# Batched experts MLP on one core: which engine waits at the end for the stores

## The chip, the cores and the metric

The kernel runs on one core of one Trainium2 chip. The metric is the device time of one execution in microseconds; a few executions of the same program are timed, and the median is given. One further execution is recorded by the hardware profiler.

A core has five engines, each with an instruction sequencer of its own: TensorE (PE: matmuls, and PEld: its weight loads), VectorE (DVE), ScalarE (ACT), GpSimd (POOL) and SyncE (SP). They run independently and wait for each other through semaphores. In the profile a "q" behind an engine's name marks an instruction that the sequencer alone handles, such as a wait; PE's are listed as PEldq.

## The reference

Eight experts, each a two-layer network with a ReLU between, on its own 256 rows:

```python
n_experts, capacity, hidden, expert_hidden = 8, 256, 512, 2048
x  : (n_experts, capacity, hidden)        float32
w1 : (n_experts, hidden, expert_hidden)   float32
w2 : (n_experts, expert_hidden, hidden)   float32

h = np.matmul(x, w1)
h = np.maximum(h, 0)
return np.matmul(h, w2).astype(np.float32)
```

## The kernel before

The kernel writes each engine's instruction stream by hand, with semaphores of its own. Weights and half of the rows are turned into bfloat16 on their way in by the DMAs that POOL issues.

**PE** first transposes the rows of x, in four rounds of 16 transposes (line 256). Then it runs a loop of four passes (line 259), two experts a pass. A pass computes the first layer of both experts (line 272), four blocks of four 128-wide slices of the 2048, and then the second layer of both (line 292), 16 slices of 128 by two halves of the 256 rows, into one PSUM tensor `pt_o`. The loop is the last thing in PE's stream.

**DVE and ACT** share the work behind PE by halves: ReLU from PSUM to `ht_sb` (lines 219 and 221), and the copy of each finished half of an expert's output from `pt_o` to `out_sb` (line 228). They report their copies on `s_dve` and `s_act`.

**POOL** issues the loads of the weights, each one expert ahead of its use as buffers come free. When the copies of the first four experts are done, it issues one store of their output (line 167, semaphore `s_out[0]`), and then drains (line 168).

**SP** issues two loads of x at the start. After that it passes the landings of the weights on to PE (lines 116 to 124). At the end it waits for the copies of experts 4 to 6 and issues one store for the three (line 126, `s_out[1]`), then for those of expert 7 and issues the last store (line 128, `s_out[2]`). At the end of the program's text, in lines 302 and 303, it waits for the landings of the three stores, each of which adds 16 to its semaphore:

```python
    for s in s_out:
        sp.wait_ge(s, 16)
```

Nothing follows in the kernel on any engine. In the built program the three waits are two instructions: one for `s_out[1]`, and one for `s_out[2]` and `s_out[0]` together. Semaphores appear in the trace by number: `s_out[0]` to `s_out[2]` are S[103] to S[105], `s_act` and `s_dve` are S[125] and S[126], and S[131] and S[132] tell ACT and DVE that a half of the second layer is complete.

The wait of line 88, which appears in the profile for PE, is in a helper, `take`, that waits for a semaphore and lowers it.

Of the kernel before, what the change touches and what calls it, by code (L numbers as in the profile page):

```python
# [9 lines left out]
def kernel(  # L10
# [74 lines left out]
    sp, pool, act, dve, pe = nc.sync, nc.gpsimd, nc.scalar, nc.vector, nc.tensor  # L85
# [214 lines left out]
                        ins.then_inc((s_ob, s_oa)[m], 1)  # L300

    for s in s_out:
        sp.wait_ge(s, 16)


# [28 lines left out]
```

## Time and profile before

| | |
|---|---|
| median of 3 runs | 179.55 us |
| lowest, highest | 179.49, 179.88 us |
| the profiled execution's own time | 179.56 us |
| its span, first to last instruction of the kernel | 178.2 us |
| PE busy | 130.0 us (73%) |
| DVE, ACT, POOL busy | 37.5, 37.9, 12.9 us |
| DMA, mean over the span | 229 GB/s |
| mean granted clock of TensorE | 0.966 |

The span is that of the kernel's own instructions, whichever engine has the first and the last. The execution's time is counted outside it and is longer. In the profile's lists a row gives the engine, the source line, the operation and the tensors (output, an arrow, inputs), then a count and times; a wait is given as who waited, an arrow, and what ended the wait. The list of DMA issues gives the KB of each and the time from issue to landing.

### The profile page before, as it was taken

The numbers are of one execution on the slowest core, as the hardware profiler recorded it, in microseconds if no ns is written. First come the engines' busy times: TensorE is split into PE (matmuls) and PEld (weight loads), VectorE is DVE, ScalarE is ACT, GpSimd is POOL, SyncE is SP. The second block draws the span as 40 slices with busy tenths as digits, with TensorE's granted clock in tenths as the row PEclk, the third lists the DMA queues.
The fourth block names the chain that finished last, engine by engine and source line by source line (L and its number), as shares of the span: only waits on it lengthen the run. The fifth ranks groups of instructions, "written<-read, shape, count | busy, mean of one in ns | idle before, by whom it ended". The sixth has DMA issues, their size and how long they took to land. (4 is left out here: it accounts for less than half of the span.)

```text
span 178.2 us, 2354 instructions
## 1 busy us (share of the span) xinstructions
PE 130.0 (73%) x824; PEld 88.8 (50%) x832; DVE 37.5 (21%) x48; ACT 37.9 (21%) x49; POOL 12.9 (7%) x27
## 2 busy tenths in 40 slices
PE   0034479898939297888769695979496698999880
PEld 0033378785414196773224485954142587964330
DVE  0134654331010133330100231320101113420110
ACT  2465554231010122130100122220101022220110
POOL 3600000101010101000000101010201200000000
PEclk9999999999999999999979999999999569999997
DMA  6999999999999998998999999999999999999998
GB/s 224 333 237 206 232 210 206 232 213 202 235 213 199 235 221 191 235 224 188 235 224 202 221 224 213 210 232 210 206 232 210 206 232 196 209 224 208 263 422 364
DMA packets 4240, 40.90 MB, mean 229 GB/s; under 512 B 400, under 2 KB 400, under 8 KB 1936
## 3 DMA queue, kind: packets, MB, share of 16 engines
q0 software_dynamic: 3408, 37.23, 95.2%
q1 hardware_dynamic: 832, 3.67, 5.2%
HBM read 71.30 MB, written 4.19 MB: 424 GB/s over the span
## 5 line engine op out<-in xcount | busy, mean ns | idle before, releaser
L272 PE MATMUL pt_h<-xe,w_sb 128*128 x512 | 65.1, 284 | 12.9 <-PEq L88 12.7
L272 PEld LDWEIGHTS pt_h<-xe,w_sb 128*128 x512 | 57.4, 147 | 21.2 <-issue 19.4
L292 PE MATMUL pt_o<-w_sb,ht_sb 128*128 x248 | 57.8, 387 | 12.5 <-PEq L88 12.1
L292 PEld LDWEIGHTS pt_o<-w_sb,ht_sb 128*128 x256 | 24.9, 99 | 44.2 <-issue 16.8
L221 DVE TENSOR_SCALAR ht_sb<-pt_h 128x512 bf16<-128x512 f32 x32 | 22.2, 693 | 52.0 <-PE pt_h L272 52.0
L219 ACT ACTIVATE ht_sb<-pt_h 128x512 bf16<-128x512 f32 x32 | 19.2, 600 | 56.9 <-PE pt_h L272 56.9
L256 PE MATMUL pt_tr<-identity,x_b 128*128 128x128 bf16 x64 | 7.5, 309 | 17.7 <-PEq L88 17.7
L228 DVE COPY out_sb<-pt_o 128x512 f32 x8 | 5.5, 692 | 67.2 <-PE pt_o L292 67.2
L228 ACT COPY out_sb<-pt_o 128x512 f32 x8 | 4.7, 585 | 65.4 <-PE pt_o L292 65.4
L256 PEld LDWEIGHTS pt_tr<-identity,x_b 128*128 128x128 bf16 x64 | 6.5, 143 | 18.4 <-issue 18.4
L132 POOL DMA_DIRECT2D w_sb<-in_w_dram x8 | 4.9, 616 | 69.9 <-ACTq L223 69.9
L198 DVE COPY xe<-pt_tr 128x1024 bf16<-128x1024 bf16 x3 | 6.2, 2077 | 8.1 <-PE pt_tr L256 8.1
L198 ACT COPY xe<-pt_tr 128x1024 bf16<-128x1024 bf16 x3 | 6.3, 2088 | 6.1 <-PE pt_tr L256 6.1
L137 POOL DMA_DIRECT2D w_sb<-in_w_dram x6 | 3.2, 536 | 36.3 <-ACT out_sb L228 36.2
L178 ACT CAST x_b<-x_f 128x1024 bf16<-128x1024 f32 x2 | 4.0, 1982 | 2.8 <-DMA x_f<-in_x_dram 2.8
L178 DVE CAST x_b<-x_f 128x1024 bf16<-128x1024 f32 x2 | 2.1, 1062 | 4.1 <-DMA x_f<-in_x_dram 4.1
L139 POOL DMA_DIRECT2D w_sb<-in_w_dram x2 | 1.1, 528 | 17.1 <-ACT out_sb L228 17.1
L178 ACT COPY x_b<-x_c 128x1024 bf16<-128x1024 bf16 x2 | 2.2, 1119 | 0.0
L178 ACT ACT_TABLE_LOAD x1 | 1.3, 1283 | 2.5 <-PEq L99 2.5
L194 DVE COPY xe<-pt_tr 128x1024 bf16<-128x1024 bf16 x1 | 0.7, 692 | 4.6 <-PE pt_tr L256 4.6
L194 ACT COPY xe<-pt_tr 128x1024 bf16<-128x1024 bf16 x1 | 1.0, 1012 | 2.0 <-PE pt_tr L256 2.0
L178 DVE COPY x_b<-x_c 128x1024 bf16<-128x1024 bf16 x2 | 1.4, 692 | 0.0
(10 smaller groups left out, 4.0 us busy)
## 6 DMA issues: line engine op xcount, KB each, us to landing
w_sb<-in_w_dram POOLq DMA_DIRECT2D x14, 2048.0 KB, 29.8
w_sb<-in_w_dram POOLq DMA_DIRECT2D x2, 1152.0 KB, 26.4
out_dram<-out_sb POOLq DMA_DIRECT2D x1, 2048.0 KB, 35.9
w_sb<-in_w_dram POOLq DMA_DIRECT2D x2, 896.0 KB, 30.2
out_dram<-out_sb SPq DMA_DIRECT2D x1, 1536.0 KB, 8.8
x_f<-in_x_dram SPq DMA_DIRECT2D x1, 1024.0 KB, 5.4
x_c<-in_x_dram POOLq DMA_DIRECT2D x1, 1024.0 KB, 9.4
x_f<-in_x_dram SPq DMA_DIRECT2D x1, 512.0 KB, 3.3
```

The costliest lines, as they stand in the source:

```text
L132: pool.dma_start(w1_k[:, e % 2 * KT1:(e % 2 + 1) * KT1], w1_r[e]).then_inc(s_w1[e], 16)
L137: pool.dma_start(w2_k[:, k:k + KT2], w2_r[e]).then_inc(s_w2[e], 16)
L139: pool.dma_start(w2_k[:, k:k + CUT], w2_r[e, :, :CUT]).then_inc(s_w2[e], 16)
L178: copy(x_b[:, b].rearrange("p (t m) q -> p t m q", m=MT), src.rearrange("p m (q t) -> p t m q", t=KT1),).then_inc(t_xb, 1)
L194: copy(xe[:, a * n:(a + 1) * n], pt[b][:].rearrange("p j q -> p (j q)")).then_inc(s_xe[b], 1)
L198: copy(xl[:, :, :, :, a - e0].rearrange("p l j q -> p j l q"), pt[b][:].rearrange("p j (l q) -> p j l q", l=l),).then_inc(s_xe[b], 1)
L219: act.activation(dst, ph[half][:], relu).then_inc(t_h, 1)
L221: dve.tensor_relu(dst, ph[half][:]).then_inc(t_h, 1)
L228: copy(outs[b], po[:, half]).then_inc(s_copied, 1)
L256: ins = pe.transpose(pt[b][:, j], x_b[:, b, j], identity[:])
L272: ins = pe.matmul(ph[i // 2][:, i % 2, :], ws[i % 2 * KT1 + kt], xs[kt], start=(kt == 0), stop=(kt == KT1 - 1),)
L292: ins = pe.matmul(po[:, m], hs[(kt - k0) * MT + m], ws[kt - k0], start=(kt == 0), stop=(kt == KT2 - 1),)
```

## The change

The waits for the landings of the three stores at the end of the program move from SP's stream to PE's. On SP the issue of the last store (line 128) is then the last instruction of the kernel; on PE the two wait instructions follow the end of the loop of line 259.

```diff
                         ins.then_inc((s_ob, s_oa)[m], 1)
 
     for s in s_out:
-        sp.wait_ge(s, 16)
+        pe.wait_ge(s, 16)
```

## The prediction

> **What bounds the kernel now.** I read the head of the profile page first, then its chain that ended last, then the waits of SP's own queue, because the change touches only what comes after the last store.
>
> ```profile
> span 178.2 us, 2354 instructions
> PE 4%; ACT 0%; issue 0%
> PE pt_o L292 4%; ACT out_sb L228 0%
> ```
>
> ```profile
> engine line waited for: us in total, times, longest us
> SPq L116 <- DMA w_sb<-in_w_dram: 87.5, 8, 20.3
> ...
> SPq L303 <- DMA out_dram<-out_sb: 4.1, 2, 3.1
> ```
>
> The chain stops at the last copy and covers only 4% of the span: it does not show the tail that matters here. The waits of SP's queue do. SP sits in line 303, the waits that the change moves, for 4.1 us in two pieces, and a DMA out of out_sb ends both. The timeline of the last stretch gives the order:
>
> ```profile
> 165.98 7.07 PE L292 MATMUL pt_o<-w_sb,ht_sb 128*128 x31 [0.79 <-PEq L88]
> 168.32 0.40 SPq L126 DMA_DIRECT2D out_dram<-out_sb  x1
> 172.87 0.69 DVE L228 COPY out_sb<-pt_o 128x512 f32 x1 [7.16 <-PE pt_o L292]
> 173.09 0.58 ACT L228 COPY out_sb<-pt_o 128x512 f32 x1 [7.27 <-PE pt_o L292]
> 173.70 0.35 SPq L128 DMA_DIRECT2D out_dram<-out_sb  x1
> ```
>
> ```profile
> out_dram<-out_sb SPq DMA_DIRECT2D x1, 1536.0 KB, 8.8
> ...
> out_dram<-out_sb SPq DMA_DIRECT2D x1, 512.0 KB, 4.5
> ```
>
> PE's last product is out at 165.98 + 7.07 = 173.05 us, the last copy at 173.67, and SP issues the last store at 173.70. It lands 4.5 us later, at 178.2, and that is the span's end. So the body of the kernel ends on a landing, and no engine that waits for it can change when it comes. Only two things are left to the change: how fast the waiting engine notices, and what follows the wait.
>
> What follows is small but not nothing. The profiled execution took 179.56 us against a span of 178.2 (178.212 in the trace), so some 1.35 us lie around the span. The views of the profile page stop at the span's end; the trace's list of semaphore updates does not. Semaphore 2, which no line of the kernel names, is updated there in two rounds of nine:
>
> ```
> S[2] round 1, us: 173.227 173.789 175.739 175.783 178.336 178.379 178.418 178.452 178.499
> S[2] round 2, us: 179.326 179.360 179.399 179.442 179.465 179.564 179.603 179.637 179.684
> between: S[207]-S[255] from 178.464, S[156]-S[206] from 178.519, S[105]-S[155] from 178.564,
>          S[54]-S[104] from 178.567, S[7]-S[53] from 178.719 to 179.067 (all set back)
> landings of the last store (S[105]): 177.880 first, 178.167 last, 16 in all
> before: S[131] 173.063 (last matmul), S[125] 173.679 (last ACT copy)
> ```
>
> I read round 1 as a closing barrier that passes through five engines and back: 173.227 comes 0.164 after PE's last matmul, 173.789 comes 0.110 after ACT's last copy, 175.739 follows the end of POOL's drain (below), 175.783 is DVE, and 178.336 is SP, after its last wait. Then four steps back. So PE stands at the head of the chain and SP at its turning point. The owners are my inference from these neighbours; the list gives no engine. [...]
>
> **The change part by part.** No transfer, copy or matmul is touched. Two sequencer instructions leave SP's end (three waits fold into two: one for the 1536 KB store, one for the other two together) and stand at PE's end.
>
> *Whom the new wait holds up.* On PE nothing of the kernel is queued behind it. In front of it stand the matmuls, and PE's sequencer is long past them:
>
> ```profile
> L259 PEldq ALU_OP  x4: 36/36/36, 55.2 to 169.2; - x4
> L259 PEldq COMPARE_BRANCH  x4: 67/214/214, 55.3 to 169.3; - x4
> ```
>
> The last loop branch is issued at 169.3, nearly 9 us before the landing, so reaching the wait costs nothing: those 9 us hide it. If the cover were gone, it would be the branch's 0.067 us. SP, once it has issued the store (173.70 + 0.35), has nothing left but its part in the barrier. POOL could be a later step in PE's chain:
>
> ```profile
> L168 POOLq DRAIN  x1: 36825/36825/36825, 138.4 to 138.4; - x1
> ```
>
> Its drain runs from 138.370 (138.4 in the row) for 36.825 us, to 175.195, and its update follows 0.544 later, at 175.739. That is 2.4 us before the last landing, so POOL is ready when PE arrives: nothing.
>
> *Noticing the landing.* The price of a wait on each sequencer, from the barrier at the start and PE's own takes:
>
> ```profile
> L303 SPq EVENT_SEMAPHORE  x2: 17/22/28, 177.1 to 178.2; - x2
> ...
> L88 PEldq EVENT_SEMAPHORE  x92: 51/51/51, 8.6 to 168.2; - x92
> ```
>
> SP's last wait begins 17 ns after the last landing (178.184 against 178.167) and takes 28 ns for two semaphores, where one takes 17. On PE one takes 51. No row has PE waiting for two: I add SP's difference, 28 - 17 = 11, for 62 (between 51 and 51 x 28/17 = 84). PE also notices later: at the start barrier a release at 0.644 begins SP's wait instruction at 0.660 and PE's at 0.673, 13 ns more. Together (62 - 28) + 13 = +47 ns, bounds +36 and +69.
>
> *From the wait to the barrier.* SP's update came 178.336 - 178.212 = 124 ns after its wait ended. For PE there are two rows: 164 ns from its last matmul to its update in round 1, where its sequencer had run ahead and only the array was late, and 179.326 - 179.067 = 259 ns from its last set-back semaphore to its update in round 2, where the sequencer itself was last. After the change the sequencer is what is late, so I take 259: 259 - 124 = +135 ns, bounds +40 and +135.
>
> *The way through the chain.* With SP last, four steps follow its update: 178.499 - 178.336 = 163 ns. With PE last, all eight follow. Round 2 is that case, as PE sets back its semaphores last: 179.684 - 179.326 = 358 ns, eight steps. So 358 - 163 = +195 ns (139 for the four steps forward; the other 56 is the turn, 99 instead of 43). It is measured, and only its place is argued; bounds +139 to +195. [...] The trace's steps are 23 to 99 ns, and the trace is used.
>
> *After the chain.* PE is the last to be let go in both cases, sets back its semaphores slowest, and opens round 2: nothing changes.
>
> Sum: 47 + 135 + 195 = +377 ns. Against the profiled execution 179.56 + 0.38 = 179.94 us. The median of the three runs, 179.55, stands 0.01 below that execution, so the forecast is 179.94 either way: slower by 0.21%. The bounds add up to 36 + 40 + 139 = +0.22 and 69 + 135 + 195 = +0.40, so 179.78 to 179.96. A measurement of this kernel can tell about 0.2%, 0.36 us, from no change: the forecast sits just over that line.
>
> **The rivals.**
>
> *PE is as quick as SP (not slower by what can be told).* [...] As a mechanism of this kernel: if the 51 ns are mostly a record that overlaps the next instruction, and the 259 ns the tail of the set-backs, only the chain is left, +0.195, and the time is 179.56 + 0.20 = 179.76. For it: PE's ordinary register operation takes 36 ns, quoted above, no triple of anything. Against: 51 ns in all 92 of its waits, to SP's 17 to 28. It decides when PE's exit takes under 240 ns, for then the sum drops below 0.36. Chance 0.17.
>
> *The rim is constant.* If what lies outside the span does not depend on who comes last (another order in the chain, or a clock that stops elsewhere), only the +47 ns inside the span remain: 179.61. For it: no view shows the rim. Against: 178.212 plus the list's 1.47 us is about the time that was counted. Chance 0.10.
>
> *A slow exit.* POOL's way from its drain's end to its update was 0.544 us. If PE, held in a wait rather than running through, needs as long in place of 259, the time is 179.94 + 0.29 = 180.23. Nothing but that row speaks for it. Chance 0.13.
>
> *Faster.* SP would have to be the slow one to leave, and its 124 ns is less than any PE row; what is left is that the stores land earlier than in this execution. The three runs' lowest lies 0.07 below the profiled one: 179.49, within the line. A gain over 0.36 us needs an earlier landing, and no edit touches a transfer. Chance 0.05.
>
> That the change does not do what it says can be left aside: the diff moves exactly the waits on the three store semaphores, and no store remains without one.
>
> **How the numbers follow.** The forecast has 0.55. With the runs' scatter (179.49 to 179.88) on top of its bounds it ends above 0.36 us in about three of four cases: 0.41 slower and 0.14 same. The slow exit adds 0.13 to slower, 0.54. Quick PE and constant rim add 0.27 to same, 0.41. Faster 0.05. The range has to hold the constant rim at 179.61 and the slow exit at 180.23: 179.6 to 180.25, which leaves out the faster case and the tails. The forecast's own range is 179.78 to 179.96.
>
> **What would show it.** In the changed kernel's profile the rows of line 303 should stand under PE's sequencer, two of them, at 51 ns or a little more, the last beginning some 30 ns after the last landing, and SP's waits for that line gone. The span should be 178.2 + 0.05 with the landing where it was. In the semaphore list round 1 should start only after the landing, with all nine updates in one run of about 0.36 us. Time outside the span should grow from 1.35 to about 1.68. I am wrong if the rim stays at 1.35, if round 1 still has its first updates at 173, or if the last store's 4.5 us to landing moves by more than the whole effect.

## The result and the profile after

The changed kernel takes 179.83 us (median of 20 runs, 179.69 to 180.09) against 179.59 for the kernel before (20 runs, 179.49 to 179.88). The ratio is 1.0014, 95% interval [1.0008, 1.002]: slower by 0.24 us. That is clear of no change in this many runs, and smaller than the 0.36 us that the prediction drew as its line.

The body of the kernel did what it did. The last stretch of the changed kernel's timeline, and the line of the last store in its list of DMA issues:

```profile
165.87 7.07 PE L292 MATMUL pt_o<-w_sb,ht_sb 128*128 x31 [0.79 <-PEq L88]
168.53 0.40 SPq L126 DMA_DIRECT2D out_dram<-out_sb  x1
172.76 0.69 DVE L228 COPY out_sb<-pt_o 128x512 f32 x1 [7.17 <-PE pt_o L292]
172.97 0.58 ACT L228 COPY out_sb<-pt_o 128x512 f32 x1 [7.27 <-PE pt_o L292]
173.58 0.35 SPq L128 DMA_DIRECT2D out_dram<-out_sb  x1
```

```profile
out_dram<-out_sb SPq DMA_DIRECT2D x1, 512.0 KB, 4.8
```

The last store is issued 0.11 us earlier than in the profile before, and lands 4.8 us later in place of 4.5. This move of 0.35 us is more than the whole effect, which the prediction had named as a sign of being wrong. It is the luck of this execution, whose own time was 180.08 us, 0.25 above the changed kernel's median: in the nine traces of this case the store is issued between 172.35 and 173.98 us, takes 4.17 to 5.77 us, and lands between 178.08 and 178.41. Comparing the two profiled executions by their ends would therefore mislead. Measured from the last landing, the luck drops out, so every reading below starts there.

Two rows by source line show that the wait moved and what it costs on PE, and that POOL's drain was over long before, at 138.3 + 37.0 = 175.3:

```profile
L303 PEldq EVENT_SEMAPHORE  x2: 51/51/51, 177.2 to 178.4; - x2
```

```profile
L168 POOLq DRAIN  x1: 36997/36997/36997, 138.3 to 138.3; - x1
```

In the waits of SP's queue no row of line 303 is left. The longest waits are these, and the waits for the weights are as before:

```profile
SPq L116 <- DMA w_sb<-in_w_dram: 87.4, 8, 20.3
SPq L103 <- DVE out_sb L228: 34.9, 5, 7.7
SPq L121 <- DMA w_sb<-in_w_dram: 34.8, 6, 9.7
```

The trace's list of semaphore updates shows the rest, as it did before:

```
changed kernel, us
last landing of the last store (S[105]): 178.405
PE's last wait: begins 178.434, ends 178.485
S[2] round 1: 178.677 178.711 178.750 178.794 178.817 178.916 178.955 178.989 179.036
S[2] round 2: 179.854 179.888 179.926 179.971 179.994 180.092 180.131 180.165 180.211
```

Round 1 no longer starts at 173. All nine updates come after the landing, in one run of 0.359 us. From the last landing to the last update of round 2 it is 180.211 - 178.405 = 1.806 us, against 179.684 - 178.167 = 1.517 before: +0.289. That tail of 0.29 and a landing that came 0.24 later account for the 0.52 us between the two profiled executions.

The counted time follows this list: the profiled execution's own time lies 0.124 us below its last update before the change, 0.131 after, and 0.114 to 0.137 in the seven experiments. So whatever delays the last update lengthens the time, although no view of the page shows these updates.

One trace of each kernel is little, but the time outside the span, in which the landing has no part, is on record for every execution (with the span to 0.1 us). Its mean is 1.57 us over the 20 of the changed kernel, and 1.32 and 1.33 over 28 and 19 executions of the kernel before, taken beside the experiments. That is +0.24 to +0.25, and the two traces give 1.595 - 1.348 = +0.25. The mean span is 178.28 us against 178.26 and 178.30.

### The profile page after: what moved, and what is told of

Read it like the earlier page. It is cut to its first block, busy times and chain, and to the rows that moved or that the text cites. A ratio compares the mean times of both kernels' runs of the same rounds, so it can differ in the third digit from the quotient of the medians.

```text
span 178.5 us, 2354 instructions
## 1 busy us (share of the span) xinstructions
PE 131.2 (74%) x824; PEld 89.7 (50%) x832; DVE 37.5 (21%) x48; ACT 37.9 (21%) x49; POOL 12.7 (7%) x27
## 5 line engine op out<-in xcount | busy, mean ns | idle before, releaser
L272 PE MATMUL pt_h<-xe,w_sb 128*128 x512 | 66.3, 288 | 11.7 <-PEq L88 11.5
L272 PEld LDWEIGHTS pt_h<-xe,w_sb 128*128 x512 | 58.3, 147 | 20.3 <-issue 17.6
```

The source lines that it names most:

```text
L272: ins = pe.matmul(ph[i // 2][:, i % 2, :], ws[i % 2 * KT1 + kt], xs[kt], start=(kt == 0), stop=(kt == KT1 - 1),)
```

## The experiments

The theory: the program ends with a barrier that passes through PE, ACT, POOL, DVE and SP and back. An engine that is late for its turn costs its own exit, and every step of the chain that then remains. Two rivals: PE costs because its sequencer is slow, wherever it stands; or SP is special, and any other engine costs the same.

**PE waits for the first two stores, SP for the last.** It undoes the part of the change that matters if order decides.

```diff
-    for s in s_out:
-        pe.wait_ge(s, 16)
+    for s in s_out[:2]:
+        pe.wait_ge(s, 16)
+    sp.wait_ge(s_out[2], 16)
```

> PE waits for the first two stores, SP alone for the last. The closing chain theory (PE heads a barrier that passes PE, ACT, POOL, DVE, SP and back; only an engine late for its turn costs, and the later its place the fewer steps follow): PE leaves its wait near 177.2, a microsecond before the last landing, the chain reaches SP before SP is free, and the time is that of before, 179.59, with the last update of semaphore 2 some 1.52 us after the last landing. The rival, that a wait on PE costs because PE leaves the kernel slowly wherever it stands, expects part of the 0.24 us that the change cost: 179.7 or more.

Measured: 179.55 against 179.54 us for the kernel before in the same runs, ratio 0.9999 [0.999, 1.0008]. PE's wait for the two earlier stores begins at 177.0 and SP's for the last at 178.2:

```profile
L303 PEldq EVENT_SEMAPHORE  x1: 51/51/51, 177.0 to 177.0; - x1
```

```profile
L304 SPq EVENT_SEMAPHORE  x1: 17/17/17, 178.2 to 178.2; - x1
```

In the list, four updates follow PE's wait and stop at SP, and five come when SP is free:

```
last landing 178.143; S[2] round 1: 177.211 177.245 177.284 177.328 | 178.295 178.339 178.377 178.411 178.458
```

The interval alone would still allow +0.14 us, a part of the 0.24. The tail does not: it is 178.143 to 179.639, 1.496 us, against 1.517 before. Nor does the time outside the span, with a mean of 1.33 us over 11 executions against 1.32 over 28. A wait on PE costs nothing as long as PE is not the last. The rival that it always costs falls.

**ACT, DVE or POOL waits in place of SP.** Three kernels, each with one word changed:

```diff
     for s in s_out:
-        sp.wait_ge(s, 16)
+        act.wait_ge(s, 16)     # second kernel: dve, third: pool
```

> ACT waits for the three stores in place of SP. Chain theory: ACT is second, so three steps forward (39 + 43 + 23 = 105 ns) and the slower turn (56 ns) come on top of SP's case, and ACT's own wait and exit cost as SP's do: +0.16 us, 179.75, and 1.68 us from the last landing to the last update of semaphore 2 (1.52 before, 1.81 with PE). Rival, PE's slow sequencer alone (51 ns a wait against ACT's and SP's 17): ACT costs nothing, 179.59. Second rival, SP is special and any other engine costs the same: +0.24 as PE, 179.83.

> DVE waits for the three stores. Chain theory: DVE stands just ahead of SP, so one step forward (23 ns) and the slower turn (56 ns) are added, and about 40 ns for its slower wait and exit: +0.12 us, 179.71, 1.64 us from the last landing to the last update. Slow-sequencer rival: a few ns (21 a wait), 179.6. SP-is-special rival: 179.83.

> POOL waits for the three stores after its drain. Chain theory with POOL's own exit as the trace of before has it (0.544 us from its drain's end to its update, 0.42 more than SP's 0.124): two steps forward (43 + 23) and the turn (56) make 0.122, so +0.54 us, 180.13, 2.06 us from the last landing to the last update. If those 0.544 us belong to the drain and not to the exit, +0.12: 179.71. SP-is-special rival: 179.83.

Measured, against 179.54 us in the same runs: ACT 179.75, ratio 1.0011 [1.0002, 1.002]; DVE 179.68, 1.0008 [0.9999, 1.0017], which by itself does not tell it from no change (the time outside the span does: a mean of 1.44 us over 11 executions against 1.32 over 28, where a single execution scatters by 0.03 to 0.04); POOL 180.15, 1.0032 [1.002, 1.0044]. The rows of line 303, in this order:

```profile
L303 ACTq EVENT_SEMAPHORE  x2: 17/28/38, 176.9 to 178.1; - x2
```

```profile
L303 DVEq EVENT_SEMAPHORE  x2: 21/36/50, 176.9 to 178.2; - x2
```

```profile
L303 POOLq EVENT_SEMAPHORE  x2: 17/30/43, 176.9 to 178.1; - x2
```

The list is the clearest picture of the case. The break (|) is where the chain stood until the last store had landed, and it moves with the engine that waits:

```
S[2] round 1, us
ACT   171.907 | 178.256 178.294 178.337 178.361 178.460 178.498 178.532 178.579
POOL  171.875 172.439 | 178.729 178.772 178.796 178.893 178.933 178.967 179.014
DVE   173.506 174.070 175.403 | 178.362 178.385 178.477 178.516 178.550 178.597
last landing: ACT 178.082, POOL 178.116, DVE 178.144
```

One update stands ahead of ACT, two ahead of POOL, three ahead of DVE, four ahead of SP, none ahead of PE. That settles the owners, which the prediction had inferred from neighbouring events. From the last landing to the last update of round 2 it is 1.685 us with ACT, 1.645 with DVE, 2.050 with POOL; expected were 1.68, 1.64 and 2.06. The 40 ns expected for DVE's slower wait and exit were the author's estimate; found were 33 in noticing and 16 in the exit, measured against SP in the trace of before. Both rivals fall on ACT: its last wait takes 38 ns, 10 more than SP's, and its exit 115 against 124, yet it cost 0.17 us in the trace; and PE's cost 0.29 there, so the engines other than SP do not cost the same. POOL, whose single wait takes 17 ns, is dearer than PE, and what is dear is its exit: 0.546 us from the end of its wait to its update. That interval was 0.544 behind its drain in the trace of before; here the drain had ended 3.3 us ahead of the wait, so the interval belongs to the exit and not to the drain.

**Both PE and SP wait for all three.** It separates what PE's wait adds from what SP's absence does.

```diff
     for s in s_out:
         sp.wait_ge(s, 16)
+        pe.wait_ge(s, 16)
```

> SP keeps its waits and PE gets the same ones as well. Chain theory: what counts is PE's late arrival at the head; SP leaves its own wait 0.17 us after the landing, before the chain reaches it (0.27 for PE's update and 0.14 for four steps after it), so its waits cost nothing: the time is that of the change, +0.24 us, 179.8, and 1.79 to 1.81 us from the last landing to the last update of semaphore 2. Rival, that it is SP's absence from the wait that costs (SP idle early, PE's wait itself free): as before, 179.55 and 1.52. Third way, the two costs add: above 180.0.

Measured: 179.90 against 179.60, ratio 1.0013 [1.0004, 1.0023], 1.776 us from the last landing (178.125) to the last update (179.901), and 0.631 to the last one of round 1, the same as in the changed kernel. The 1.776 is 0.014 under what was expected; the difference arises after round 1. SP's wait beside PE's costs nothing:

```profile
L303 SPq EVENT_SEMAPHORE  x2: 17/22/28, 176.9 to 178.1; - x2
```

```profile
L304 PEldq EVENT_SEMAPHORE  x2: 51/51/51, 176.9 to 178.2; - x2
```

**Four more instructions behind the waits, on PE and on SP.** It sizes the exit, the term that the prediction was least sure of. The increments are of a semaphore that nobody reads; in the built program the first of them joins the wait for the two earlier stores, so four instructions stand behind the wait for the last.

```diff
     for s in s_out:
         pe.wait_ge(s, 16)          # other kernel: sp
+    for _ in range(4):
+        pe.sem_inc(s_extra, 1)     # other kernel: sp
```

> As the change, but four semaphore increments follow PE's waits (the increments are of a semaphore that nobody reads), so that some four more instructions stand between the landing and PE's leaving. Chain theory: PE's exit is on the path whole, and an instruction on PE's sequencer behind a wait has stood 100 to 151 ns behind the one before: +0.4 to +0.6 us over the change, 180.2 to 180.4, 2.2 to 2.4 us from the last landing to the last update. If only the 51 ns that the record gives a wait count: +0.2, 180.0, 2.0 us. If the exit overlaps something else: nothing, 179.8, 1.81.

> As the kernel before, but with four increments of an idle semaphore behind SP's waits. Chain theory: SP's exit is on the path whole, and SP's instructions at its end stood 53 to 66 ns apart: +0.21 to +0.26 us over before, 179.8, 1.73 to 1.78 us from the last landing to the last update, as much as the move to PE cost. If only the 17 ns of the record count: +0.07, 179.6, 1.59.

Measured: on PE 180.43 against 179.60 us, ratio 1.0043 [1.0027, 1.006], 2.383 us from the last landing to the last update. On SP 179.82, ratio 1.0009 [1.0, 1.0019], 1.766 us. Both tails and SP's time are in the range that the chain theory gave; PE's time lies 0.03 us above it. For SP the interval reaches down to no change, so there the trace carries the reading: 1.766 us against 1.517. The rows of the added instructions, PE's and SP's:

```profile
L306 PEldq EVENT_SEMAPHORE  x4: 51/51/51, 178.3 to 178.7; - x4
```

```profile
L306 SPq EVENT_SEMAPHORE  x4: 17/17/28, 178.2 to 178.4; - x4
```

On PE the four start, in the trace, at 178.251, 178.400, 178.551 and 178.701, so one takes 150 ns of the sequencer although the row says 51. On SP they begin 59 to 70 ns apart, with 17 to 28 in the row. SP stays at the turning point of the chain here, and the four instructions still cost nearly what the whole move to PE cost, +0.22 us against +0.24: the exit of the last engine lies on the path whole.

All kernels side by side, in ns from the trace: the last landing to the end of the last wait (or of the last added instruction), from there to the engine's update, and the landing to the last update of each round. Then, in us, the mean time outside the span over all executions (the added instructions lie inside the span) and the medians' difference to the kernel before.

| last engine | noticing | exit | to end of round 1 | to end of round 2 | outside the span | time |
|---|---|---|---|---|---|---|
| SP (before) | 45 | 124 | 332 | 1517 | 1.32, 1.33 | |
| PE (the change) | 80 | 192 | 631 | 1806 | 1.57 | +0.24 |
| SP, PE for two stores | 33 | 119 | 315 | 1496 | 1.33 | +0.01 |
| ACT | 59 | 115 | 497 | 1685 | 1.47 | +0.21 |
| DVE | 78 | 140 | 453 | 1645 | 1.44 | +0.14 |
| POOL | 67 | 546 | 898 | 2050 | 1.85 | +0.61 |
| PE, SP waits too | 79 | 193 | 631 | 1776 | 1.60 | +0.30 |
| PE, four more | 641 | 239 | 1238 | 2383 | 1.63 | +0.83 |
| SP, four more | 281 | 139 | 582 | 1766 | 1.36 | +0.22 |

From the end of round 1 to that of round 2 it is 1.145 to 1.192 us in every kernel, whoever was late. The means outside the span agree with the traces' own (time less span) within 0.03 us, so the single traces are not exceptions.

## Why the prediction was right, and which term was off

The mechanism is the one forecast, and the range and the direction held. The size was too large: +0.38 us was forecast and +0.29 found in the traces, and +0.24 between the medians. The time of 179.83 lies inside the forecast's own range of 179.78 to 179.96. By the prediction's line of 0.36 us, though, the outcome is "within 0.2%", to which it gave 0.41, and not "slower by over 0.2%", to which it gave 0.54. Term by term:

- *Body, cover, SP's and POOL's part: nothing.* Right. PE's first wait began only when the store of three experts had landed, at 177.2, and POOL (drain over at 175.3) and SP (last store issued by 173.93) stood ready.
- *Noticing: +47 forecast.* Found 80 - 45 = +35, just below its lower bound of 36. PE noticed 29 ns after the landing (17 + 13 = 30 forecast), but its wait for two semaphores takes 51 ns like any other; the 11 ns added by analogy with SP were not there.
- *Exit: +135 forecast.* Found 192 - 124 = +68. This is the step that was mis-sized. The prediction chose between two rows, 164 and 259 ns, and took 259, from PE's last set-back semaphore to its update in round 2. The true value lies 28 above the lower row and 67 below the upper one. In the three kernels where PE leaves behind a plain wait (the change, the split, both) its exit took 192 to 198 ns, and behind an added increment 239. So what PE's sequencer did last seems to change the exit, and the row behind set-back semaphores did not stand for a wait. Nor is that row steady: it is 259 ns in five of the nine traces and 224 in the other four, the change among them. What makes these differences, no record names. A part of PE's exit may be the wait itself: in the trace of before, the sequencer's next instruction of its own (a weight load left out) begins 150 to 197 ns after a wait has begun whose row says 51, in 91 of the 92 waits of line 88. That is an argument; no run here separates it.
- *The chain: +195 forecast.* Found 359 - 163 = +196.
- *After the chain: nothing.* Right within 10 ns: 1.175 us from the end of round 1 to that of round 2, against 1.185. So close a match is luck, since this stretch differs by up to 47 ns between the kernels.

35 + 68 + 196 - 10 = +289 ns. About two thirds of it are the chain's order, one third is PE's slowness.

The rivals: "PE is as quick as SP" was to be decided by PE's exit taking under 240 ns, and it took 192. So the sum stays under 0.36 us, as that rival said, and the measured 179.83 lies nearer to its 179.76 than to the forecast's 179.94. Its mechanism, no price of PE's own, fell all the same: noticing and exit together cost 35 + 68 = 103 ns more on PE than on SP, of the 182 that were forecast. The increments behind the waits show the same: one started 150 ns behind the other on PE, and 59 to 70 on SP.

"The rim is constant" fell: outside the span it grew from 1.35 us to 180.08 - 178.49 = 1.59 (1.68 was forecast). "A slow exit" fell for PE, and is true of POOL.

The mean of the eight steps of the changed kernel's closing barrier is 359 / 8 = 45 ns. Four added steps at that mean would be 180 ns, an estimate; the change added 196. Of these the four steps forward are 140 and the turn 56: it took 99 ns in the changed kernel, where the chain ran through, and 43 in the kernel before, where the chain had waited there.

What remains open: what each engine does in its exit (nothing between the wait and the update is recorded), and why the time between the rounds varies by 0.047 us; 0.035 of this stands between the last set-back semaphore and round 2, in the row of 224 or 259 ns above. No version here beats the kernel before; the split one equals it.

## What to carry to other kernels

This kernel ends on the landing of a store, and the wait for it was cheapest on the engine whose turn in the closing barrier comes last, SP: on DVE it cost 0.14 us more, on ACT 0.21, on PE 0.24 and on POOL 0.61. Nothing should stand behind that wait: four instructions there lengthened the way from the last landing to the last update by 2.383 - 1.806 = 0.58 us on PE and by 1.766 - 1.517 = 0.25 on SP. An engine ahead in the chain could wait for what lands earlier: PE did, from 177.0 us with the last landing at 178.143, at no cost (179.55 us against 179.54). Whether the order is the same in other programs, no run here shows; the list of semaphore updates in its trace would. To read such an effect, measure from the last landing in the trace, since the landing itself moved by more than the effect: 178.08 to 178.41 us in the nine traces, against 0.24.

## What the runs showed of the hardware

- In the nine traces the closing barrier runs PE, ACT, POOL, DVE, SP and back. Run through, it took 0.356 to 0.363 us (round 1 of three traces, round 2 of all nine); from SP alone, 0.162 to 0.163.
- The record's duration of a semaphore instruction is not its price. Added increments show 51 ns on PE and start 149 to 151 ns apart; on SP they show 17 to 28 and start 59 to 70 apart.
- In the record a wait for two semaphores took longer than one for a single semaphore on ACT (38 ns against 17), DVE (50 against 21), POOL (43 against 17) and SP (28 against 17), and no longer on PE (51).
- From the end of a plain wait to the engine's update POOL took 0.546 us, the other engines 0.115 to 0.198.
